# Four columns of an adaptive-norm modulation: dot products on VectorE replaced by matmuls on TensorE

## The chip, the cores and the metric

The kernel runs on one core of a Trainium2 chip. The metric is the device time of one execution in microseconds (us). A core has a matrix engine (TensorE, PE in the rows, with its weight loads shown apart as PEld), a vector engine (VectorE, DVE), a scalar engine (ScalarE, ACT), GpSimd (POOL) and a queue engine that issues most transfers (SyncE, SP).

## The reference, cut to what matters

One block of a hybrid network over 256 tokens of width 2048: a modulated norm, a large input projection, two mixers, an output projection and a feed-forward part, all in float32. What the change touches is the modulation:

```python
mod = jnp.einsum('bd,de->be', jax.nn.silu(c), w_ada[l]) + b_ada[l]      # c: [1, 2048], w_ada: [2048, 12288]
sh1, sc1, gt1, sh2, sc2, gt2 = jnp.split(mod[:, None, :], 6, axis=-1)
h = rms_norm(x, norm1_g[l]) * (1.0 + sc1) + sh1
proj = jnp.einsum('btd,dc->btc', h, w_in[l])
```

So `mod` is a vector of 12288 numbers, each a dot product of length 2048. The kernel holds it as 96 columns of 128 (`modc`, 128x96): column j (0 to 15) is `sh1` for the j-th 128 rows of the transposed activations, and column 16 + j is `sc1` for the same rows.

## The kernel before, in words

The program is written with tiles; a planner orders the instructions of each engine by a priority and by its own timeline, and each engine then runs its queue in that order. What is written under `START` comes first in priority, then the stream of weights (`STREAM`), then the rest (`MAIN`).

**Start.** `c` is loaded as one row (`crow`), spread over 128 partitions by four float32 matmuls of one row (`cps`), and turned into `sb`, a 128x2048 tile of twice silu(c), by a tanh on ScalarE and a multiply on VectorE. `x` comes transposed in four transfers (`xn`); its squares (`sqs`) are summed by float32 matmuls into `pss`, and four short VectorE steps make the reciprocal root `rs`.

**The modulation.** A column e of `modc` is one transfer of 1 MB (128 rows of the transposed `w_ada`, 8 KB each) into a slot of `ap`, and one VectorE instruction over 128x2048 elements (`ada_long`, L170 for the transfer, L158 for the dot) that multiplies by `sb` and sums. The first four columns, 0, 16, 1 and 17, have four slots of `ap` to themselves; later ones take two of these slots in turn.

**Rounds.** The input projection for 4448 of the columns of `w_in` goes in five rounds over the rows of h: rows 0 and 1 (of 16 groups of 128), then 2 and 3, then 4 to 7, and so on, so that the projection of a round needs only the columns of `modc` of its own rows. A round first makes `am` from the scale columns, then `modulate` makes each row group's `hf` on VectorE, `hhi` on ScalarE (its rounded high part) and `hlo` on VectorE (the rest), and nine groups of columns of `w_in` follow. Each step of a group loads a piece of 512 KB (`wr`, four slots), splits it into a high part on ScalarE (`whi`) and a low part on VectorE (`wlo`, three slots each), and runs three matmuls for each 128x128 tile: high by high, high by low, low by high. Between the steps the columns of `modc` for the next round are made (`next_ada`), their transfers in the same SyncE queue as the weights.

Later parts (both mixers, output projections, feed-forward) are not touched.

The lines that the change replaces, and the helper that makes a column:

```python
    rounds = [(0, 2), (2, 2), (4, 4), (8, 4), (12, 4)]
    for j in range(rounds[0][1]):
        ada_long(j)
        ada_long(16 + j)
```

Of the kernel before, what the change touches and what calls it, by code (L numbers as in the profile page):

```python
# [13 lines left out]
AF = mybir.ActivationFunctionType  # L14
OP = mybir.AluOpType
# [3 lines left out]
D = 2048  # L19
# [4 lines left out]


P_BADA, P_N1, P_N2, P_MU, P_A0, P_KK, P_KA, P_RK, P_LNW, P_LNB = 0, 96, 112, 128, 155, 163, 171, 179, 187, 195
P_QG, P_KG0, P_KG1, P_KG2, P_PEK, P_PEV, NPRM = 203, 204, 205, 206, 207, 223, 239

C_ID, C_MSK, C_HS, C_ONE, C_BLK, C_CUM, C_SEL, NCST = 0, 128, 192, 224, 225, 353, 609, 737

# [2 lines left out]
def block_kernel(ctx, tc, a):  # L33
    nc = tc.nc
# [28 lines left out]
    def B16(name, shape, dt=FT):  # L63
        return b16.tile(shape, dt, name=name, tag="b16")
# [4 lines left out]
    def RAW(name, shape):  # L69
        return rawp.tile(shape, FT, name=name, tag="raw")  # L70

    def T2(name, shape, dt=FT):
        return t2.tile(shape, dt, name=name, tag="t2")
# [4 lines left out]
    def PX(name, shape=(128, 512)):  # L78
        return px.tile(list(shape), FT, name=name, tag="px")

    def PM(name, shape=(128, 512)):
        return pmm.tile(list(shape), FT, name=name, tag="pm")
# [35 lines left out]
    xT = a["xT"].rearrange("(k p) t -> p k t", p=128)  # L118
# [4 lines left out]
    prm = cst.tile([128, NPRM], FT, name="prm")  # L123
# [8 lines left out]
    modc = cst.tile([128, 96], FT, name="modc")  # L132
# [10 lines left out]
    for i in range(4):  # L143
        ps = PM("cps")
# [11 lines left out]
    def ada_dot(r, s, start, out):  # L156
        with behind():
            V.tensor_tensor_reduce(out=r, in0=r, in1=s, scale=0.5, scalar=start,  # L158
                                    op0=OP.mult, op1=OP.add, accum_out=out)

    apb = [B16("ap0", [128, 2, D]), B16("ap1", [128, 2, D])]
    apn = [0]
    SLOTS = 2

    def ada_long(e):

        n = apn[0] if apn[0] < 4 else apn[0] % SLOTS
        r = apb[n // 2][:, n % 2]
        apn[0] += 1
        nc.sync.dma_start(r, a["w_ada_t"][e * 128:(e + 1) * 128])  # L170
        ada_dot(r, sb, prm[:, P_BADA + e:P_BADA + e + 1], modc[:, e:e + 1])
# [8 lines left out]
                    modc[:, e:e + 1] if h else part)  # L180

    rounds = [(0, 2), (2, 2), (4, 4), (8, 4), (12, 4)]
    for j in range(rounds[0][1]):
        ada_long(j)
        ada_long(16 + j)


    def split(raw, hi, lo):
# [20 lines left out]
    def parts(name, x):  # L209
        n = x.shape[0]  # L210
        r = [T2(name, [n, 512], FR) for _ in range(2)]
        split(x, r[0], r[1])
        return r
# [25 lines left out]
    def proj(segs_of, W, ms, rhi, rlo, kps, evac, banks=None, first=True, last=True):  # L239


        nb = (len(ms) + 1) // 2
        ps = banks or [PM("pp") for _ in range(nb)]
        for i, kp in enumerate(kps):
            hi, lo = weights(segs_of(kp), W)
            next_ada(ada_long if starting[0] else ada)
            todo = [[(k, m) for m in range(len(ms))] for k in range(2)]
            if 0 and i == len(kps) - 1 and nb == 2:
                todo = [[(k, m) for k in range(2) for m in range(len(ms)) if m // 2 == b] for b in range(2)]
            for part in todo:  # L250
                for k, m in part:
                    (c0, cw), kc = ms[m], 2 * kp + k
                    o = ps[m // 2][0:cw, (m % 2) * 256:(m % 2) * 256 + 256]
                    mm3(o, hi[:, k, c0:c0 + cw], lo[:, k, c0:c0 + cw], rhi[:, kc], rlo[:, kc],
                        first and i == 0 and k == 0 and m % 2 == 0, last and i == len(kps) - 1 and k == 1)
                yield
        if evac:
            with prio(STREAM):
                for b in range(nb):
                    evac(b, ps[b])  # L260
# [70 lines left out]
    w_in = a["w_in"]  # L331

    def wseg(cols):
        def of(kp):
            out, c = [], 0
            for c0, w in cols:
                out.append((w_in[kp * 256:(kp + 1) * 256, c0:c0 + w], c, w))
                c += w
            return out
        return of  # L340
# [8 lines left out]
    def acc_evac(dst, first, last):  # L349
        def f(b, ps):  # L350
            d, rows, store = dst(b)
            s = ps[0:rows, 0:d.shape[1] * 256].rearrange("p (m t) -> p m t", t=T)
            if first:
                S.copy(d, s)
            else:
                tt(d, d, s, OP.add)
            if last and store is not None:
                nc.gpsimd.dma_start(store, d)
        return f
# [4 lines left out]
    for i in (2, 3):  # L364
        groups.append(([(i * 512, 512)], 512, M4,
                       lambda b, i=i: (prk[:, i // 2, (i % 2) * 4 + 2 * b:(i % 2) * 4 + 2 * b + 2], 128, None), None))
    for i in range(2):
        groups.append(([(2048 + i * 512, 512)], 512, M4, None, pvp[2 * i:2 * i + 2]))
    for i in range(2):
        groups.append(([(i * 512, 512)], 512, M4,  # L370
                       lambda b, i=i: (prk[:, i // 2, (i % 2) * 4 + 2 * b:(i % 2) * 4 + 2 * b + 2], 128, None), None))
# [7 lines left out]
    for r, (j0, n) in enumerate(rounds):  # L379
# [9 lines left out]
        for cols, W, ms, dst, banks in groups:  # L389
            g = proj(wseg(cols), W, ms, hhi, hlo, range(j0 // 2, (j0 + n) // 2),  # L390
                     dst and acc_evac(dst, first, last), banks, first or banks is None, last or banks is None)
# [81 lines left out]
    ps = PX("gnp")  # L473
# [10 lines left out]
    for j in range(8):  # L484
        i, h = j // 4, j % 4
# [4 lines left out]
    for t in range(2):  # L490
        for h in range(2):
            ps = PX("zps")
            mm(ps, twa[:, t * 128:t * 128 + 128], w2a[:, h * 512:h * 512 + 512])
            th, cols = T2("th", [128, 512]), slice(h * 512, h * 512 + 512)
# [7 lines left out]
    for j in range(8):  # L502
        ps = PX("gps")
# [22 lines left out]
    for jp in range(4):  # L526
        ps = PX("aps")
        for i in range(2):
            j = 2 * jp + i
            mm(ps[:, i * T:i * T + T], a2[64:128, j * 128:j * 128 + 128], pl[64:128, 0], i == 0, i == 1)  # L530
        for i in range(2):
            j = 2 * jp + i
# [3 lines left out]
    ps = PX("kss")  # L536
    for jp in range(4):
        sq = T2("ksq", [128, 512])
        for i in range(2):
            j = 2 * jp + i  # L540
# [8 lines left out]
    for jp in range(4):  # L549
        ps = PX("knb")  # L550
        spread(ps, jp, nr)
        for i in range(2):
            j = 2 * jp + i
# [24 lines left out]
    for jp in range(4):  # L578
        for hh in range(2):
            ps = PX("lps")  # L580
            r0 = hh * 64
            for i in range(2):
                j = 2 * jp + i
# [19 lines left out]
    for jp in range(4):  # L603
        pb = T2("pb", [128, 2, T])
        for i in range(2):
            j = 2 * jp + i
            stt(pb[:, i], pr8[:, j], prm[:, P_RK + j:P_RK + j + 1], pk8[:, j], OP.mult, OP.mult)
        ps = PX("bps")
# [20 lines left out]
    for t in range(2):  # L629
        for jq in range(2):  # L630
            ps = PX("vps")
# [8 lines left out]
    for j in range(8):  # L640
        ps = PX("xps")
# [10 lines left out]
    for j in range(8):  # L652
        ps = PX("bkp")
# [59 lines left out]
    for c in range(8):  # L713
# [7 lines left out]
        if c:  # L721
            for hh in range(2):
                ps = PX("zps")
# [5 lines left out]
        for hh in range(2):  # L729
            ps = PX("ups")  # L730
# [5 lines left out]
        if c < 7:  # L736
            ps = PX("hps")
# [46 lines left out]
    ps = PX("fps")  # L784
# [23 lines left out]
    for jp in range(4):  # L808
        ps, pg = PX("ytp"), PX("gtp")
        ya = T2("ya", [128, 2, T])  # L810
        for i in range(2):
            j = 2 * jp + i
            for t in range(2):
                PE.transpose(ps[:, i * T + t * 128:i * T + t * 128 + 128], yn[:, t, j * 128:j * 128 + 128], ident)
        for i in range(2):
            j = 2 * jp + i
            mm(pg[:, i * T:i * T + T], g2[:, 0, j * 128:j * 128 + 128], pl[:, 1], i == 0, False)
            mm(pg[:, i * T:i * T + T], g2[64:96, 1, j * 128:j * 128 + 128], pl[64:96, 2], False, True)
        for i in range(2):
            j = 2 * jp + i  # L820
# [17 lines left out]
    ps = PX("kp")  # L838
# [4 lines left out]
    r = T2("krr", [64, 512])  # L843
    rsqrt(r, ps[0:64], 1.0 / 64, 1e-6, T2("krt", [64, 512]))
    r = parts("krp", r)
    for b in range(2):
        ps = PX("kb")
# [4 lines left out]
    for src in range(2):  # L852
        for dst in range(2):
            o = kc[dst * 64:dst * 64 + 64, src:4:2].rearrange("p g b t -> p b g t")
            i = kr[src * 64:src * 64 + 64, 4:8].rearrange("p (b g) t -> p b g t", b=2)
# [32 lines left out]
    ps = PX("c1p")  # L888
# [13 lines left out]
    ps = PX("c2p")  # L902
# [4 lines left out]
    ps, ps2 = PX("c3p"), PX("c4p")  # L907
# [12 lines left out]
    ps = PX("c5p")  # L920
# [20 lines left out]
    ps = PX("scp")  # L941
# [18 lines left out]
    ps = PX("pct")  # L960
# [132 lines left out]
    ps = PX("ss2")  # L1093
# [25 lines left out]
    for g in range(16):  # L1119
        ps = [(PM if g % 2 else PX)("pu") for _ in range(4)]  # L1120
        for kp in range(8):
# [5 lines left out]
            for k, m in order:  # L1127
                kc, c = 2 * kp + k, slice(m * 128, m * 128 + 128)
                r = h2[kc // 8][:, :, kc % 8]
                mm(ps[m].rearrange("p (x t) -> p x t", x=2), hi[:, k, c], r, kc == 0, False)  # L1130
                mm(ps[m][:, T:2 * T], lo[:, k, c], r[:, 0], False, kc == 15)
        with prio(STREAM):
            for b in range(2):
                m = 4 * g + 2 * b
                r = T2("relu", [128, 2, T])
                for i in range(2):
                    p = ps[2 * b + i]
# [5 lines left out]
    for t in range(2):  # L1143
        for q in range(4):
            ps = PX("xtp")
# [12 lines left out]
    for kp in range(32):  # L1158
# [4 lines left out]
        for k, h in ([(0, 0), (0, 1), (1, 0), (1, 1)] if kp < 31 else [(0, 0), (1, 0), (0, 1), (1, 1)]):  # L1163
                kc = 2 * kp + k
                with prio(STREAM):
                    r = RAW("wd", [128, 1024])
# [44 lines left out]
def _pack(inp):  # L1211

    g = {k: v[0] if k != "rel_bias" else v for k, v in inp.items()}
    p = np.zeros((128, NPRM), np.float32)

    def cols(at, v):
        v = v.reshape(-1, 128)
        p[:, at:at + v.shape[0]] = v.T

    cols(P_BADA, g["b_ada"])  # L1220
    cols(P_N1, g["norm1_g"])
    cols(P_N2, g["norm2_g"])
    cols(P_MU, g["rwkv_mu"][:3328])
    p[64:96, P_MU + 26] = g["rwkv_mu"][3328:]
    for at, k in ((P_A0, "rwkv_a0"), (P_KK, "rwkv_k_k"), (P_KA, "rwkv_k_a"), (P_LNW, "rwkv_ln_w"), (P_LNB, "rwkv_ln_b")):
        cols(at, g[k])
    cols(P_RK, g["rwkv_r_k"].reshape(-1))
    for at, v in ((P_QG, g["q_norm_g"]), (P_KG0, g["k_norm_g"][0]), (P_KG1, g["k_norm_g"][1]), (P_KG2, g["k_norm_g"][2])):
        p[:, at] = np.concatenate([v, v])
    for at, k in ((P_PEK, "cmp_pe_k"), (P_PEV, "cmp_pe_v")):  # L1230
        p[:, at:at + 16] = g[k].reshape(16, 2, 64).transpose(1, 2, 0).reshape(128, 16)
    c, onehot = _consts()
    out = {
        "xT": g["x"].T, "c": g["c"], "w_ada_t": g["w_ada"].T, "w_in": g["w_in"], "params": p, "consts": c,
        "onehot": onehot, "w2a": np.concatenate([g["rwkv_w2"], g["rwkv_w0"][None]]), "a2": g["rwkv_a2"],
        "g2": g["rwkv_g2"], "w1k": g["cmp_w1_k"], "w2k": g["cmp_w2_k"], "w1v": g["cmp_w1_v"], "w2v": g["cmp_w2_v"],
        "rel_bias": g["rel_bias"], "w_o_rwkv": g["w_o_rwkv"], "w_o_nsa": g["w_o_nsa"], "w_out": g["w_out"],
        "w_up": g["w_up"], "w_down": g["w_down"],
    }
    return {k: np.ascontiguousarray(v) for k, v in out.items()}  # L1240
# [17 lines left out]
```

## Time and profile before

| what | value |
|---|---|
| median of 3 runs | 1659.62 us (1655.1 to 1662.33) |
| the profiled execution | 1666.43 us, of which the span from first to last instruction is 1664.7 us |
| PE busy in the span | 1587.8 us (95%) |
| PEld busy | 1404.8 us (84%) |
| DVE busy | 1150.9 us (69%) |
| ACT busy | 757.1 us (45%) |
| mean granted TensorE clock | 0.977 of full |

Busy times are sums of the durations of an engine's instructions. Matmuls overlap in the record, so the spacing of their starts tells their rate and the duration of one does not. Only the first stretch of the span, up to some 170 us, differs from a steady flow of matmuls, and the change lies within it.

### The profile page before, as it was taken

What the parts mean: (1) busy time and instruction counts of PE and PEld (TensorE: products, weight loads), DVE (VectorE), ACT (ScalarE), POOL (GpSimd) and SP (SyncE); (2) the same over time, 40 slices, a digit from 0 to 9 for tenths busy, and PEclk for the clock granted to TensorE, in tenths of its full rate; (3) what the DMA queues carried; (4) which work ended last, traced back from release to release, by engine and by line L of the source; (5) the groups of instructions that cost most, each with busy time, mean ns of one, the idle gap of its engine ahead of it and who ended that gap; (6) DMA issues with size and microseconds to landing.
All of it is one profiled execution on the core that took longest, in us unless ns stands there. A gap on an engine that the chain in (4) does not pass through costs nothing.

```text
span 1664.7 us, 28125 instructions
## 1 busy us (share of the span) xinstructions
PE 1587.8 (95%) x11286; PEld 1404.8 (84%) x11286; DVE 1150.9 (69%) x1696; ACT 757.1 (45%) x1111; POOL 35.6 (2%) x60
## 2 busy tenths in 40 slices
PE   5969999899999989999999799999989999999998
PEld 4968998789899879877999688888878888888886
DVE  7999876977778666777876767666645555555545
ACT  4423458527323265656534444444334544444442
POOL 0000000000000000000000000000000000000001
PEclk9989999997999999999999899999999999999999
DMA  9999767674868677754787477777776556556554
GB/s 366 318 330 344 242 185 235 214 219 159 273 215 265 211 242 258 249 176 155 261 292 265 140 250 243 261 246 247 246 181 187 199 195 195 191 195 194 192 192 149
DMA packets 171190, 381.99 MB, mean 229 GB/s; under 512 B 29281, under 2 KB 43921, under 8 KB 166706
## 3 DMA queue, kind: packets, MB, share of 16 engines
q1 hardware_dynamic: 149344, 355.79, 65.4%
q0 software_dynamic: 4192, 14.17, 2.4%
q10 hardware_dynamic: 17523, 10.24, 2.1%
q8 instruction: 88, 1.44, 0.4%
q14 instruction: 43, 0.35, 0.1%
HBM read 370.13 MB, written 10.01 MB: 228 GB/s over the span
## 4 chain that ended last, share of the span: by engine, by line
PE 68%; DMA 14%; DVE 10%; ACT 3%; issue 3%; ACTq 0%; DVEq 0%; SPq 0%
PE pp L99 20%; PE pu L99 18%; PE da L99 10%; PE db L99 10%; DMA ar<-in_w_ada_t 4%; DVE wlo L90 4%; DMA wr<-in_w_in 3%; DMA wr<-in_w_out 2%; DMA wr<-in_w_up 2%; PE pvp L99 2%; ACT whi L189 1%; DVE ap L158 1%; PE y L99 1%; DVE ar L158 1%; DMA kx<-skv 1%
## 5 line engine op out<-in xcount | busy, mean ns | idle before, releaser
L189 ACT CAST whi<-wr 128x1024 fp32r<-128x1024 f32 (+1 forms) x352 | 367.1, 1044 | 522.1 <-PE pp L99 129.4
L90 DVE TENSOR_TENSOR wlo<-wr,whi 128x1024 fp32r<-128x1024 f32 (+1 forms) x352 | 426.0, 1215 | 184.8 <-ACT whi L189 181.5
L99 PE MATMUL pp<-hhi,whi 128*128 128x256 f32 (+1 forms) x1072 | 309.7, 292 | 22.1 <-ACT hhi L87 21.6
L99 PE MATMUL pp<-hhi,wlo 128*128 128x256 f32 (+1 forms) x1072 | 302.6, 290 | 6.8 <-DVE wlo L90 6.6
L99 PE MATMUL pp<-hlo,whi 128*128 128x256 f32 (+1 forms) x1072 | 307.1, 288 | 0.2 <-DVE hlo L93 0.2
L90 DVE TENSOR_TENSOR wdl<-wd,wdh 128x1024 fp32r<-128x1024 f32 x128 | 156.6, 1225 | 171.6 <-ACT wdh L189 171.6
L99 PEld LDWEIGHTS pp<-hhi,whi 128*128 128x128 f32 (+1 forms) x1072 | 209.2, 196 | 30.9 <-ACT hhi L87 22.8
L189 ACT CAST wdh<-wd 128x1024 fp32r<-128x1024 f32 x128 | 134.9, 1055 | 193.6 <-PE db L99 188.6
L99 PEld LDWEIGHTS pp<-hhi,wlo 128*128 128x128 f32 (+1 forms) x1072 | 206.0, 195 | 14.4 <-DVE wlo L90 9.7
L99 PEld LDWEIGHTS pp<-hlo,whi 128*128 128x128 f32 (+1 forms) x1072 | 209.5, 195 | 3.9 <-issue 2.7
L99 PE MATMUL pu<-h2b,whi 128*128 128x512 f32 x512 | 179.8, 399 | 4.1 <-ACT whi L189 4.1
L99 PE MATMUL pu<-h2a,whi 128*128 128x512 f32 x512 | 178.1, 399 | 4.4 <-DVE h2a L93 4.4
L99 PE MATMUL pu<-h2b,wlo 128*128 128x256 f32 x512 | 140.8, 282 | 0.5 <-DVE wlo L90 0.5
L99 PE MATMUL pu<-h2a,wlo 128*128 128x256 f32 x512 | 137.3, 282 | 0.0
L158 DVE CUSTOM_DVE_ANT_0 ar<-ar,sb,prm 128x1024 f32<-128x1024 f32 x64 | 82.0, 1282 | 67.4 <-DMA ar<-in_w_ada_t 67.4
L99 PEld LDWEIGHTS pu<-h2b,whi 128*128 128x128 f32 x512 | 96.6, 190 | 26.5 <-ACT whi L189 4.4
L99 PEld LDWEIGHTS pu<-h2a,whi 128*128 128x128 f32 x512 | 95.7, 190 | 26.1 <-DVE h2a L93 5.2
L99 PEld LDWEIGHTS pu<-h2b,wlo 128*128 128x128 f32 x512 | 96.8, 191 | 2.0 <-DVE wlo L90 1.3
L99 PEld LDWEIGHTS pu<-h2a,wlo 128*128 128x128 f32 x512 | 96.3, 191 | 2.3 <-DVE wlo L90 0.3
L158 DVE CUSTOM_DVE_ANT_0 ar<-ar,sb,adap 128x1024 f32<-128x1024 f32 x64 | 82.0, 1282 | 16.7 <-DMA ar<-in_w_ada_t 16.2
L99 PE MATMUL db<-wdl,uh 128*128 128x512 f32 x256 | 79.6, 389 | 0.0
L99 PE MATMUL db<-wdh,ul 128*128 128x512 f32 x256 | 79.6, 389 | 0.0
(336 smaller groups left out, 2747.6 us busy)
## 6 DMA issues: line engine op xcount, KB each, us to landing
wr<-in_w_in SPq DMA_DIRECT2D x136, 512.0 KB, 5.3
ar<-in_w_ada_t SPq DMA_DIRECT2D x128, 512.0 KB, 4.8
wr<-in_w_up SPq DMA_DIRECT2D x128, 512.0 KB, 4.3
wd<-in_w_down SPq DMA_DIRECT2D x128, 512.0 KB, 4.3
ap<-in_w_ada_t SPq DMA_DIRECT2D x32, 1024.0 KB, 7.0
wr<-in_w_out SPq DMA_DIRECT2D x32, 512.0 KB, 5.2
wr<-in_w_in SPq DMA_DIRECT2D x40, 256.0 KB, 3.7
wr<-in_w_o_rwkv SPq DMA_DIRECT2D x16, 512.0 KB, 4.4
```

What stands on the lines that cost most here:

```text
L90: return V.tensor_tensor(out, x, y, op=op).ins
L99: PE.matmul(out, l, r, start=start, stop=stop, skip_group_check=True)
L158: V.tensor_tensor_reduce(out=r, in0=r, in1=s, scale=0.5, scalar=start, op0=OP.mult, op1=OP.add, accum_out=out)
L189: S.copy(hi, raw)
```

## The change

The transfer of the transposed `w_ada` rows for columns 0, 16, 1 and 17 and the VectorE dots on them are replaced. The host lays the same part of `w_ada` out anew (`w_ada_p`): for each of the four columns a 128x2048 block whose 16 pieces of 128x128 have the contraction on the partitions. `c` is also put into the parameter tile as 16 columns of 128; a tanh and a multiply make `scc` (128x16), twice silu(c), with the contraction on the partitions. For each column 16 float32 matmuls follow, each with one 128x128 piece as the stationary operand and one column of `scc` as the moving one, summed in one bank of PSUM (`adp`); a VectorE instruction halves the sum and adds the bias. The transfers keep their size and their slots; `sb` is still made, as all the other columns use it.

```diff
-    for j in range(rounds[0][1]):
-        ada_long(j)
-        ada_long(16 + j)
+
+    scc = T2("scc", [128, 16])
+    act(scc, prm[:, P_C:P_C + 16], AF.Tanh, scale=0.5)
+    stt(scc, scc, 1.0, prm[:, P_C:P_C + 16], OP.add, OP.mult)
+    for i, e in enumerate((0, 16, 1, 17)):
+        r = apb[i // 2][:, i % 2]
+        apn[0] += 1
+        nc.sync.dma_start(r, a["w_ada_p"][i * 128:(i + 1) * 128])
+        ps = PX("adp")
+        for k in range(16):
+            mm(ps[:, 0:1], r[:, k * 128:k * 128 + 128], scc[:, k:k + 1], k == 0, k == 15)
+        stt(modc[:, e:e + 1], ps[:, 0:1], 0.5, prm[:, P_BADA + e:P_BADA + e + 1], OP.mult, OP.add)
...
+    cols(P_C, g["c"])
...
+        "w_ada_p": np.concatenate([g["w_ada"][:, e * 128:(e + 1) * 128].reshape(16, 128, 128).transpose(1, 0, 2).reshape(128, D)
+                                   for e in (0, 16, 1, 17)]),
```

## Rows read from the trace of the kernel before

**Rows 1.** The page, part 1: busy time, share of the span and instructions per engine.

```profile
PE 1587.8 (95%) x11286; PEld 1404.8 (84%) x11286; DVE 1150.9 (69%) x1696; ACT 757.1 (45%) x1111; POOL 35.6 (2%) x60
```

**Rows 2.** Timeline of the first 30 us: start, duration, engine, instruction, [idle before <-releaser].

```profile
2.89 7.16 PE L99 MATMUL cps<-crow,one 1*128 1x512 f32 x8 [2.89 <-DMA crow<-in_c]
...
13.66 2.34 DVE L158 CUSTOM_DVE_ANT_0 ap<-ap,sb,prm 128x2048 f32<-128x2048 f32 x1
...
16.67 2.08 PE L99 MATMUL pss<-sqs,cs 128*128 128x256 f32 x4 [6.62 <-DVE sqs L90]
...
21.88 2.34 DVE L158 CUSTOM_DVE_ANT_0 ap<-ap,sb,prm 128x2048 f32<-128x2048 f32 x1
...
25.28 0.15 DVE L93 SCALAR_TENSOR_TENSOR am<-modc,prm 128x2 f32<-128x2 f32 x1
...
27.90 1.22 PE L99 MATMUL pp<-hhi,whi 128*128 128x256 f32 x4 [9.15 <-ACT hhi L87]
...
29.28 0.58 PE L99 MATMUL pp<-hlo,whi 128*128 128x256 f32 x1 [0.16 <-DVE hlo L93]
```

**Rows 3.** DMA issues around 5.4 and 8.9 us: count, KB each, us to landing.

```profile
ap<-in_w_ada_t SPq DMA_DIRECT2D x1, 1024.0 KB, 7.5
...
ap<-in_w_ada_t SPq DMA_DIRECT2D x1, 1024.0 KB, 11.3
```

**Rows 4.** Timeline of SyncE: first issue of four, and the fourth of them alone.

```profile
5.34 3.74 SPq L170 DMA_DIRECT2D ap<-in_w_ada_t  x4
...
8.75 0.33 SPq L170 DMA_DIRECT2D ap<-in_w_ada_t  x1
```

**Rows 5.** Timeline near 653 us: 16 float32 matmuls with 32 moving columns.

```profile
653.14 3.66 PEld L99 LDWEIGHTS scp<-kcb,qn 128*128 128x128 f32 x32
```

**Rows 6.** The chain that ended last, 382 to 408 us: start, length, engine, count.

```profile
388.46 6.97 PE xps L99 x128
395.43 3.60 PE bkp L655 x16
...
405.62 1.75 PE bkp L655 x16
```

**Rows 7.** Stretches of 3.4 us: PE, PEld, DVE, ACT, POOL busy (instructions), clock, DMA share, GB/s.

```profile
382.63:386.05 3.42, 3.22 (x60) 3.21 (x61) 3.14 (x9) 3.34 (x6) 0.00 (x0) 0.50 0.02 5
...
389.46:392.87 3.41, 3.41 (x68) 3.41 (x66) 3.07 (x11) 3.30 (x7) 0.00 (x0) 0.50 0.02 5
```

**Rows 8.** Timeline of PEld: weight loads of 128x128 at 31.6 us and at 35.0 us.

```profile
31.38 0.33 PEld L99 LDWEIGHTS pp<-hhi,wlo 128*128 128x128 f32 x1
31.59 0.33 PEld L99 LDWEIGHTS pp<-hhi,whi 128*128 128x128 f32 x1
...
35.01 0.19 PEld L99 LDWEIGHTS pp<-hhi,whi 128*128 128x128 f32 x1
35.13 0.19 PEld L99 LDWEIGHTS pp<-hlo,whi 128*128 128x128 f32 x1
```

**Rows 9.** The chain that ended last around 94 us, from `am` to the first matmul.

```profile
93.98 0.17 DVE am L93
...
95.26 15.55 PE pp L99 x112
```

**Rows 10.** The chain that ended last, 29 to 92 us.

```profile
45.01 13.31 PE pp L99 x111
59.03 1.87 DVE ap L158
...
86.08 5.48 DMA ap<-in_w_ada_t
```

**Rows 11.** Longer stretches, columns as in rows 7.

```profile
20.00:28.00 8.00, 0.10 (x1) 0.10 (x1) 7.97 (x14) 3.53 (x5) 0.00 (x0) 1.00 1.07 417
...
80.00:120.00 40.00, 26.58 (x204) 26.07 (x204) 37.78 (x46) 10.88 (x13) 0.00 (x0) 0.83 0.92 327
120.00:200.00 80.00, 75.88 (x621) 74.58 (x620) 74.33 (x88) 30.48 (x35) 0.00 (x0) 1.00 0.89 307
```

More of the change, by code (lines that the diff above doesn't have):

```diff
@@ L26 @@
 P_BADA, P_N1, P_N2, P_MU, P_A0, P_KK, P_KA, P_RK, P_LNW, P_LNB = 0, 96, 112, 128, 155, 163, 171, 179, 187, 195
-P_QG, P_KG0, P_KG1, P_KG2, P_PEK, P_PEV, NPRM = 203, 204, 205, 206, 207, 223, 239
+P_QG, P_KG0, P_KG1, P_KG2, P_PEK, P_PEV, P_C, NPRM = 203, 204, 205, 206, 207, 223, 239, 255
 C_ID, C_MSK, C_HS, C_ONE, C_BLK, C_CUM, C_SEL, NCST = 0, 128, 192, 224, 225, 353, 609, 737
@@ L1233, in _pack @@
     out = {
-        "xT": g["x"].T, "c": g["c"], "w_ada_t": g["w_ada"].T, "w_in": g["w_in"], "params": p, "consts": c,
+        "xT": g["x"].T, "c": g["c"], "w_ada_t": g["w_ada"].T,
+        "w_ada_p": np.concatenate([g["w_ada"][:, e * 128:(e + 1) * 128].reshape(16, 128, 128).transpose(1, 0, 2).reshape(128, D)
+                                   for e in (0, 16, 1, 17)]),
+        "w_in": g["w_in"], "params": p, "consts": c,
         "onehot": onehot, "w2a": np.concatenate([g["rwkv_w2"], g["rwkv_w0"][None]]), "a2": g["rwkv_a2"],
```

## Prediction, made before the changed kernel was timed

> **What bounds the kernel now.** I read the page's busy shares first: PE is busy 95% of the span, VectorE 69% [rows 1]. That is an average, and the change lies wholly in the first stretch, so I went on to the timeline of the first 30 us. TensorE does its four one-row matmuls, then the four passes of `pss`, and apart from these nothing until 27.90 us, where it has waited 9.15 us for `hhi` [rows 2]. The reader is to see what stands before `hhi`: a row of VectorE dots of 2.34 us each, the first at 13.66, the fourth from 21.88 to 24.2, then `am` at 25.28, then `hf`, `hhi`, matmul [rows 2]. VectorE is busy 7.97 of the 8 us from 20 to 28 and the transfers run at 417 GB/s [rows 11].
>
> Next the landings of the four tiles of `w_ada`, which the change keeps: the first is issued at 5.34 and lands 7.5 us later, at 12.84; the fourth is issued at 8.75 and lands 11.3 us later, at 20.05 [rows 3, 4]. So the fourth dot ends some 4.1 us after its data are there: VectorE, not the transfer, sets the start of the projection, but by no more than that.
>
> Last the chain that ended last. From 29 to 58.3 us it is TensorE, then VectorE with the dots of later columns, with transfers between them (5.48 us at 86.08) until 95 us [rows 10]. From 80 to 120 us PE is busy 26.58 of 40 us while VectorE is busy 37.78 and the DMA share is 0.92 [rows 11]; from 120 to 200 PE has 4.1 us idle. A delay at the start is thus not wholly added: some of it could be taken from these gaps, if VectorE and the queue get ahead in the meantime.
>
> **Part by part: what is removed.** Four dots: 4 x 2.34 = 9.4 us of VectorE [rows 2]. None of them lies beside TensorE work; they are the path to `hhi`. The transfers stay, same size and same slots, as do `sb` and the sums for `rs`.
>
> **What is added beside other work.** `scc` needs only the parameter tile, and takes one short tanh and one short multiply of 16 columns; both can run before the first tile lands at 12.84, so I put them at nothing. If they were late, the first matmul of a column would be late by their length, under 1 us. The four sums in PSUM cost VectorE an instruction on one column each, which I price like `am`, 0.15 us [rows 2]; the first three are hidden under the next column's matmuls.
>
> **What is added on the path: 64 float32 matmuls.** Each appears as two pairs of weight load and matmul: `pss` is two matmuls in the program and x4 in the row [rows 2], `scp` 16 in the program and x32 [rows 5]. So 64 matmuls are 128 passes, each with a full 128x128 load, while only one column moves. No such matmul is in the trace. From below: `scp`, with 32 moving columns, takes 3.66 us for 32 passes, 0.114 us a pass [rows 5], at a granted clock of 1.00. From above: the transposes `bkp`, one load of 128x128 and 128 moving columns each, take 3.60 us for 16, 0.225 us, at a granted clock of 0.50, and 1.75 us, 0.109 us, in the second group, at 1.00 [rows 6, 7]. So the whole question is the clock.
>
> Low: 128 x 0.114 = 14.6 us. High: 128 x 0.225 = 28.8 us. Either way a column takes longer (3.6 or 7.2 us) than the tiles take to arrive one after the other (7.2 us for three steps, 2.4 each [rows 3, 4]), so the matmuls start at 12.84 and run on without waiting for data.
>
> I take the high end, for three rows. The projection itself starts at the low level: loads of 128x128 stand 0.21 us apart and last 0.33 us at 31.6 us, 0.12 apart and 0.19 us at 35.0 [rows 8]; the clock column prints 1.00 already for 20 to 28 us [rows 11], so there the spacing tells the level. The 7.16 us of `cps` before that, dense but with one row, had not raised it [rows 2]. And in three stretches of 3.4 us from 382.6 to 392.9 us, the first and last shown, PE is busy 3.22 and 3.41 us, PEld as well, with small matmuls, and the granted clock stays at 0.50, the 1.2 GHz level [rows 7]. A stream of loads with one moving column each looks more like these than like the dense projection that does raise it. A load that lasts 0.33 us at the low level and 0.19 us at the high one [rows 8] also says that loads follow the clock.
>
> A page speaks for the other end. The Trainium skill (TensorE: Matmul & The Clock Gate, LDWEIGHTS) gives a weight load as its columns divided by 1.2, in ns, 107 ns for 128 columns, with no clock in it. By that 128 passes would take 13.7 us, an estimate from the page, and rival "fast loads" below would hold. Rows 5 agree with it at a clock of 1.00; rows 8 speak against it at the low level.
>
> **The sum.** First landing 12.84; 128 passes at 0.225, 28.8 us: 41.6. The four passes of `pss` (2.08 us [rows 2]) share TensorE's queue; their data come after the first tile, so I count them in between: 43.7. Then the last sum's VectorE instruction, 0.15, and from `am` to the first matmul 95.26 - 93.98 = 1.28 us [rows 9]: 45.1 us. Before, this matmul stood at 27.90 [rows 2]: 17 us later; 15 if `pss` goes behind the wait of something else.
>
> What waits behind. Engines run their queues in order. The last sum's instruction stands in VectorE's queue; the `hf`, the `wlo` and the dots of columns 2 and 18 that the planner put behind it wait until 43.7 us, though their transfers have landed. ScalarE's `hhi` holds back the `whi` behind it. SyncE's next weights wait for a free slot of `wr`, the next columns for the two slots of `ap`. So most of the wait isn't used to get ahead. What is gained back: after the wait the transfers no longer run at their limit of 417 GB/s [rows 11], the next weights lie there, and the part from 58 to 95 us, where VectorE sets the chain [rows 10], starts with fewer transfers outstanding. I take 4.5 us of the 17 back, between 0 and 9 (two thirds of the 13.4 us that PE idles from 80 to 120 [rows 11], since VectorE, busy 37.78 us there, keeps the rest). Net: 17 - 4.5 = 12.5 us.
>
> The profiled execution took 1666.43 us, span 1664.7, 6.8 us above the median of 1659.62. The sum is a difference, so I put it on the median: 1659.6 + 12.5 = 1672.
>
> **Rivals.**
>
> "Slow loads" is the forecast: the low clock throughout, the queues blocked. +8 to +18 us, 1668 to 1677.
>
> "Slow loads, used wait": the same 28.8 us, but the planner has put the `wlo` and the next dots ahead of the last sum, so that VectorE and the queue are a round's work ahead when TensorE starts, and the idle 13.4 us of 80 to 120 [rows 11] is filled. For it: PE is not the bound there. Against: the slots of `wr`, `whi` and `wlo` hold only a few pieces. 17 - 12 = +5: 1665.
>
> "Fast loads": the clock rises under the narrow matmuls, or the load isn't slowed by it. 12.84 + 14.6 + 1.0 (`pss` at that rate) + 1.4 = 29.9 against 27.90, +2; if the clock is up when the projection starts, the 5 us or so that it now spends at 0.21 a matmul go at 0.12 [rows 8], -2.2. Together about 0, from -3 to +3: 1660. For it: at 1.00 the rate is on record [rows 5]. Against: rows 7. The Trainium skill (the same page, Part 1) says that the throttled state is the default and that sustained activity, not a number of matmuls, releases it; by that the clock would rise within the first column and this rival holds. Rows 7 show PE kept busy at 0.50, so here activity alone isn't enough.
>
> "VectorE relieved", the other side: faster. It needs the matmuls to keep pace with the landings, a pass under 2.4 / 32 = 0.075 us; then the last column is ready at 20.05 + 2.4, the first matmul at 24.0, 4 us earlier; the clock gives 2.2, and the VectorE time freed up to 28 us moves the splits ahead by 2 to 3. -9 us: 1651. For it: VectorE has no idle time in that stretch [rows 11] and loses 9.4 us of work. Against: the fastest full load on record is 0.109 us.
>
> **How the numbers follow.** Slow loads 0.56, slow loads with a used wait 0.14, fast loads 0.24, VectorE relieved 0.06. The likeliest gives 1672, its own range 1668 to 1677. The bound of 0.5% is 8.3 us, 1651.3 to 1667.9, about what a measurement of this kernel tells from no change. Slower: nearly all of slow loads, 0.55. Faster: 0.07. Same: 0.38. For 8 in 10 the range must reach into fast loads; I leave out its lower part, relieved VectorE, and what a changed order of the planner may add on top: 1657 to 1680.
>
> **What would show it.** In the timeline, 128 weight loads `adp`, 0.21 to 0.23 us apart, from 12.8 to about 42 us; the wait before the first `pp` at 44 to 46 us, put down to `hhi`; VectorE idle before it; in the chain, `adp` in place of the dots. The loads at 0.11 apart, or a first `pp` before 32 us, would make the forecast wrong; so would a first `pp` at 45 with PE's idle time from 60 to 170 us gone. If the span grows by far more than 17 us, the cause is elsewhere: a new order of the queues further on.

## The result and the profile after

The changed kernel takes 1680.35 us (median of 4 runs, 1677.54 to 1685.87) against 1657.44 us for the kernel before (median of 4, 1655.1 to 1662.33): a ratio of 1.0125, with a 95% interval of 1.0093 to 1.0157. It is slower by 22.9 us, or 1.25%.

The page's busy shares, for [rows 1]:

```profile
PE 1605.6 (96%) x11414; PEld 1424.2 (85%) x11414; DVE 1142.6 (68%) x1693; ACT 756.8 (45%) x1112; POOL 35.6 (2%) x60
```

PE has 128 instructions and 17.8 us more, VectorE 8.3 us less. The timeline of the first 56 us (columns as in [rows 2]) shows where they lie:

```profile
13.51 27.38 PEld L99 LDWEIGHTS adp<-scc,ap 128*128 128x128 f32 x128 [5.19 <-DVE sqs L90]
13.54 27.44 PE L99 MATMUL adp<-scc,ap 128*128 128x1 f32 x128 [3.64 <-DVE sqs L90]
...
28.74 2.35 DVE L158 CUSTOM_DVE_ANT_0 ap<-ap,sb,prm 128x2048 f32<-128x2048 f32 x1
...
34.27 2.34 DVE L158 CUSTOM_DVE_ANT_0 ap<-ap,sb,prm 128x2048 f32<-128x2048 f32 x1
...
40.84 2.05 PE L99 MATMUL pss<-sqs,cs 128*128 128x256 f32 x4
41.02 0.16 DVE L93 SCALAR_TENSOR_TENSOR modc<-adp,prm 128x1 f32<-128x1 f32 x1 [4.40 <-PE adp L99]
41.09 2.34 DVE L158 CUSTOM_DVE_ANT_0 ap<-ap,sb,prm 128x2048 f32<-128x2048 f32 x1
...
44.23 2.35 DVE L158 CUSTOM_DVE_ANT_0 ap<-ap,sb,prm 128x2048 f32<-128x2048 f32 x1
...
47.42 0.42 DVE L93 SCALAR_TENSOR_TENSOR rs<-rs,rst 128x256 f32<-128x256 f32 x1
48.26 2.35 DVE L158 CUSTOM_DVE_ANT_0 ap<-ap,sb,prm 128x2048 f32<-128x2048 f32 x1 [0.42 <-DMA ap<-in_w_ada_t]
...
50.53 1.67 DVE L93 SCALAR_TENSOR_TENSOR hf<-xn,am,rs 128x256 f32<-128x256 f32 x4
51.05 1.71 ACT L87 ACTIVATE hhi<-hf,modc 128x256 fp32r<-128x256 f32 x4 [7.19 <-DVE hf L93]
...
51.61 1.22 PE L99 MATMUL pp<-hhi,whi 128*128 128x256 f32 x4 [8.71 <-ACT hhi L87]
...
54.93 0.58 PE L99 MATMUL pp<-hlo,whi 128*128 128x256 f32 x1 [2.10 <-DVE hlo L93]
```

The reader is to see three things. The 128 passes take 27.38 / 128 = 0.214 us each and run without a gap, though the tiles have long landed. `pss`, which the norm needs, stands behind all of them (40.84, before 16.67 [rows 2]), so `rs` is ready only at 47.8. And VectorE, free again at 41.2, first does three dots of later columns, which stand ahead of `hf` in its queue; two more were done beside the passes, from 28.7 and 34.3 us, so that five dots of later columns are behind it when the projection starts, where the kernel before has done none. The first matmul of the projection comes at 51.61 instead of 27.90 [rows 2]: 23.7 us later.

How much of that is left later? I read both kernels at three marks: the first `pp`, the last `aps` (a small matmul just behind the projection's rounds), and the first `ss` (the second norm, behind both mixers and the output projections). Each kernel has two profiled executions here, the second from the experiments below.

| kernel | first `pp` | last `aps` | first `ss` | `aps` to `ss` | span |
|---|---|---|---|---|---|
| before | 27.90 | 277.5 | 930.4 | 652.9 | 1664.7 |
| before, second | 28.19 | 280.7 | 926.8 | 646.1 | 1658.1 |
| changed | 51.61 | 289.8 | 946.3 | 656.5 | 1675.8 |
| changed, second | 51.85 | 291.6 | 948.8 | 657.2 | 1683.3 |

In the means of the pairs the changed kernel is 23.7 us late at the first `pp`, 11.6 at the last `aps`, 19.0 at `ss` and 18.2 at the end. So half of the delay is made up within the projection, and 7.3 us come on top in the mixers, a stretch that differs by 6.8 us between the two executions of the kernel before. That the medians lie 23 us apart and these spans 18 is the spread of the executions: the first profile of before took 1666.43 us, 9 above its median.

How the half is made up shows in the stretch from the first `pp` to 170 us (columns as in [rows 7]), here of the kernel before:

```profile
27.90:170.00 142.10, 123.65 (x968) 121.22 (x969) 131.39 (x150) 52.77 (x66) 0.00 (x0) 0.95 0.94 335
```

and of the changed one:

```profile
51.61:170.00 118.39, 110.51 (x873) 108.64 (x873) 115.30 (x133) 48.46 (x62) 0.00 (x0) 0.99 0.96 342
```

PE idles 142.10 - 123.65 = 18.5 us before and 7.9 us after. The granted clock is 0.95 and 0.99 there; both figures leave out the low level at the start of the projection, which the column prints as 1.00. The projection starts later but has fewer holes, and above all it lacks one: the wait for `hhi` at the start of the third round, which in the kernel before is (PE's waits from 52 to 170 us: total us, times, longest)

```profile
PE pp L99 <- ACT hhi L87: 12.4, 1, 12.4
```

and 14.6 us in its second execution. In the changed kernel no wait of PE from 60 to 170 us is longer than 3.5 us in either execution.

The mixers' stretch has the same matmuls in both, but more PE idle time. Of the second execution of before:

```profile
280.70:926.80 646.10, 625.79 (x5830) 561.88 (x5828) 484.95 (x906) 311.81 (x531) 26.20 (x46) 0.98 0.72 231
```

and of the changed kernel:

```profile
291.60:948.80 657.20, 626.85 (x5831) 563.82 (x5830) 483.87 (x906) 310.99 (x530) 26.21 (x46) 0.97 0.71 227
```

20.3 us idle against 30.4, with the busy times of PE and of VectorE equal within 1.1 us. The amount of work is the same; what differs is waiting.

### The profile page after: what moved, and what is told of

It reads as the page before. It is cut to its first block, busy times and chain, and to the rows that moved or that the text cites. A ratio compares the mean times of both kernels' runs of the same rounds, so it can differ in the third digit from the quotient of the medians.

```text
span 1675.8 us, 28381 instructions
## 1 busy us (share of the span) xinstructions
PE 1605.6 (96%) x11414; PEld 1424.2 (85%) x11414; DVE 1142.6 (68%) x1693; ACT 756.8 (45%) x1112; POOL 35.6 (2%) x60
## 4 chain that ended last, share of the span: by engine, by line
PE 62%; issue 22%; DMA 8%; DVE 6%; ACT 2%; POOL 1%; SPq 0%; DVEq 0%; ACTq 0%; POOLq 0%
PE pu L99 19%; PE pp L99 14%; PE da L99 10%; PE db L99 10%; DMA ar<-in_w_ada_t 2%; PE pvp L99 2%; DVE wlo L90 2%; DMA wr<-in_w_out 2%; PE adp L99 2%; DVE ap L158 1%; PE po L99 1%; ACT whi L198 1%; DMA wr<-in_w_up 1%; PE sps L99 1%; DMA gate<-sma 1%
## 5 line engine op out<-in xcount | busy, mean ns | idle before, releaser
L158 DVE CUSTOM_DVE_ANT_0 ar<-ar,sb,adap 128x1024 f32<-128x1024 f32 x64 | 81.8, 1278 | 17.8 <-DMA ar<-in_w_ada_t 17.5
```

## Experiments

All ratios are against the kernel before on the same chips, whose median was 1656.5 to 1658.7 us there. Each kernel was timed beside its own runs of the kernel before, so two of them are best compared by their ratios.

**Half of the pieces.** The sum over 8 of the 16 pieces, so half of it is left out.

```diff
-        for k in range(16):
-            mm(ps[:, 0:1], r[:, k * 128:k * 128 + 128], scc[:, k:k + 1], k == 0, k == 15)
+        for k in range(8):
+            mm(ps[:, 0:1], r[:, k * 128:k * 128 + 128], scc[:, k:k + 1], k == 0, k == 7)
```

> Each of the four columns is summed from 8 of its 16 pieces, so half of the sum is left out; transfers, slots and all other instructions stay. Theory A (the matmuls lie on the path to the projection, 0.214 us for each of 128 passes): 64 passes fewer, adp ends near 27 us instead of 41, the first pp at 37 to 40 us instead of 51.6, and the time falls by 10 to 14 us from 1680, to about 1667 to 1670. Theory B (the loss comes from the new order of the instructions behind the start, as the planner makes another one for any change): the time stays near 1680 or moves by an amount that has nothing to do with the 13.7 us.

1674.68 us, 1.0098 (1.0069 to 1.0126): 5.7 us less than the changed kernel by the medians and 4.5 by the ratios, with intervals that overlap; not 10 to 14. The first `pp` came at 37.96, 13.7 us earlier, as theory A has it; the last `aps` at 285.4, only some 5 us earlier. So a microsecond at the start is worth less than half of one at the end of the projection. Theory A holds for the start and falls for the size at the end; theory B alone can't explain an `aps` that moves with the start.

**`pss` ahead.** The loop of matmuls and its four VectorE instructions are moved, in the program, behind the matmuls of `pss`; the transfers stay.

```diff
     for k in range(2):
         mm(pss, ones, sqs[:, k], k == 0, k == 1)
+    for i, e in enumerate((0, 16, 1, 17)):
+        r = apb[i // 2][:, i % 2]
+        ps = PX("adp")
...
```

> The matmuls of the four columns are written behind pss, so that pss goes ahead of them in TensorE's queue; nothing is left out. Theory A1 (the order around the matmuls costs beside the matmuls: pss behind all 128 passes and three dots of later columns ahead of hf): rs is ready near 20 us, the first pp at 43.5 to 45.5 us instead of 51.6, the time falls by 4 to 7 us, to about 1675. Theory A0 (only the 27.4 us of passes count, what stands around them is made up later): the first pp is earlier, the time stays within 2 us of 1680.

1674.47 us, 1.0099 (1.0074 to 1.0123). First `pp` at 45.76, last `aps` at 284.8. The order around the matmuls cost 6 us at the first `pp` and 5 to 7 at the last `aps`, theory A1; of the whole time 4 us by the ratios, with intervals that overlap. Three dots of later columns were done before the first `pp`, and the wait of the third round is gone, as in the changed kernel. The mixers' stretch is 660.8 us.

**Dots behind, too.** As above, and every later dot is issued behind the `hlo` of the first round.

```diff
-        with behind():
+        with (tc.issue_after(first_h[0]) if first_h else behind()):
             V.tensor_tensor_reduce(out=r, in0=r, in1=s, scale=0.5, scalar=start,
...
             lasth = modulate(j0, n, xn)
             if first:
+                first_h.append(lasth)
```

> As the one with pss ahead, and the VectorE dots of all later columns are also issued behind hlo of the first round; nothing is left out. Theory A1: first pp near 44 us and the dense projection near 45.5, time 1672 to 1675, as the sum of the prediction has it. Theory C (the dots done during the wait are what the kernel lives from later, the used wait): with them moved behind, the first matmul is as early but the time is no better than with pss ahead alone, 1675 or more.

1670.07 us, 1.0081 (1.0055 to 1.0108). Its timeline is the sum of the prediction nearly row for row:

```profile
43.36 0.16 DVE L93 SCALAR_TENSOR_TENSOR modc<-adp,prm 128x1 f32<-128x1 f32 x1 [6.67 <-PE adp L99]
43.55 0.16 DVE L93 SCALAR_TENSOR_TENSOR am<-modc,prm 128x2 f32<-128x2 f32 x1
...
44.83 1.22 PE L99 MATMUL pp<-hhi,whi 128*128 128x256 f32 x4 [1.51 <-ACT hhi L87]
```

But the wait is now unused. From 30 to 60 us (columns as in [rows 7]; the clock column prints 1.00 although the passes in this stretch have the price of the low level):

```profile
30.00:60.00 30.00, 28.49 (x176) 28.41 (x177) 15.14 (x19) 7.70 (x12) 0.00 (x0) 1.00 0.51 185
```

VectorE is busy 15.14 us and the transfers run at 185 GB/s; with `pss` ahead alone the same stretch has

```profile
30.00:60.00 30.00, 26.91 (x142) 26.39 (x143) 21.64 (x29) 6.61 (x12) 0.00 (x0) 1.00 0.80 284
```

What wasn't done then is missing later: the wait for `hhi` of the third round is back,

```profile
PE pp L99 <- ACT hhi L87: 11.8, 1, 11.8
```

and the last `aps` comes at 293.1 instead of 284.8. That is theory C, as far as the projection goes. The time is no worse all the same (1.0081 against 1.0099, with intervals that overlap), because the mixers' stretch is 649.4 us here and 660.8 there. Theory A1 came out for the first matmul, theory C for the projection, and neither for the time: 1672 to 1675 and 1675 or more were expected.

**Only `scc`.** The parameter columns and `scc` stay, the dots come back.

```diff
-    for i, e in enumerate((0, 16, 1, 17)):
...
+    for j in range(rounds[0][1]):
+        ada_long(j)
+        ada_long(16 + j)
```

> scc, the 16 extra parameter columns and their two instructions are there, but the four columns are made by VectorE dots as before; nothing is left out. Theory A: within 3 us of the kernel before, 1655 to 1662, first pp near 28 us. Theory B (any change of the start re-plans the rest and that alone costs): 1665 or more although the first pp is as early as before.

1660.81 us, 1.0023 (1.0003 to 1.0044), first `pp` at 26.70, `aps` to `ss` 649.6. A new plan that begins alike costs some 4 us here, by the interval 0.5 to 7; that is a little more than theory A's 3 us, and theory B by itself isn't the 23.

**Dense matmuls ahead, to raise the clock.**

```diff
+    wj = PM("wj")
+    for i in range(8):
+        mm(wj, ident, xn[:, 0:2], True, True)
     for i, e in enumerate((0, 16, 1, 17)):
```

> Eight dense float32 matmuls of 128x128 by 512 columns, whose result nobody reads, stand between cps and the first matmul of the four columns; all else stays. They take TensorE from about 10 to about 20 us and so start the four columns some 6 us later. Theory L (the pass takes 0.214 us because the clock is low; a load follows the clock): the clock rises in the dense matmuls, the passes then take 0.11 us as long as it stays up, adp ends at 34 to 36 us instead of 41, and the time falls by 2 to 4 us from 1680. Theory N (0.214 us is the price of a load with one moving column at any clock): adp ends near 47, time 1683 to 1687. In between, if one moving column can't hold the clock up: the first passes at 0.11, the later ones at 0.214.

1677.33 us, 1.0107 (1.0070 to 1.0145). Weight loads of `adp` in two windows, 19 to 24.5 and 25.5 to 41 us (min/median/max ns, first and last start):

```profile
L99 PEld LDWEIGHTS adp<-scc,ap x49: 190/192/192, 19.1 to 24.5; 128*128 128x128 f32 x49
...
L99 PEld LDWEIGHTS adp<-scc,ap x74: 333/333/333, 25.4 to 40.9; 128*128 128x128 f32 x74
```

and the stretches, with the granted clock as third number from the end:

```profile
22.00:24.00 2.00, 2.00 (x20) 2.00 (x19) 0.92 (x2) 1.09 (x2) 0.00 (x0) 1.00 1.04 386
24.00:25.00 1.00, 1.00 (x9) 1.00 (x10) 0.36 (x2) 0.73 (x1) 0.00 (x0) 0.83 1.05 387
25.00:26.00 1.00, 1.00 (x6) 1.00 (x6) 0.99 (x1) 0.96 (x1) 0.00 (x0) 0.50 1.12 430
...
30.00:40.00 10.00, 10.00 (x49) 10.00 (x48) 5.88 (x6) 0.00 (x0) 0.00 (x0) 0.50 0.80 299
```

Until 24.5 us a pass takes (24.5 - 19.1) / 48 = 0.113 us at a clock of 1.00; then the clock falls to 0.50, the 1.2 GHz level, in the midst of passes that leave PE and PEld no idle time, and a pass takes (40.9 - 25.4) / 73 = 0.212 us. The expectation's third case came: the price is that of the clock, and this stream of loads with one moving column didn't hold the clock up. Theory N falls. `adp` ended at 41, no later than without the dense matmuls, although it began 5 us later. The first `pp` came at 54.24, as three dots of later columns stand ahead of `hf` here too, and the last `aps` at 295.2; the time differs from that of the changed kernel by less than the intervals.

**One column by matmul.** Column 0 only, the other three by dots, `pss` ahead.

```diff
-    for i, e in enumerate((0, 16, 1, 17)):
-        r = apb[i // 2][:, i % 2]
-        apn[0] += 1
-        nc.sync.dma_start(r, a["w_ada_p"][i * 128:(i + 1) * 128])
...
+    r0 = apb[0][:, 0]
+    apn[0] += 1
+    nc.sync.dma_start(r0, a["w_ada_p"][0:128])
+    for e in (16, 1, 17):
+        ada_long(e)
...
```

> Only column 0 is made by matmuls (32 passes), columns 16, 1 and 17 by VectorE dots as before; pss is ahead of the matmuls; nothing is left out. Theory A (what counts is how late the first pp is): 32 passes end near 24 us, beside the dots, so the first pp stands at 26 to 28.5 us as before and the time is within 3 us of the kernel before, 1655 to 1661. Theory B (a new order of the rest costs by itself): 1665 or more with the first pp as early as before.

1653.63 us, 0.9973 (0.9953 to 0.9993): faster than the kernel before, and below both theories. So I timed it again:

> The one-column kernel unchanged, timed again against the kernel before. Theory G (its lead of 0.3% is real): 1650 to 1656, ratio under 1 with its interval again. Theory Z (it was chance): 1655 to 1660, interval around 1.

1654.30 us in 12 runs, 0.9971 (0.9951 to 0.9990). Theory G: the lead of 0.3% is real. The timeline of the second:

```profile
16.78 7.16 PEld L99 LDWEIGHTS adp<-scc,ap 128*128 128x128 f32 x32
...
21.99 2.34 DVE L158 CUSTOM_DVE_ANT_0 ap<-ap,sb,prm 128x2048 f32<-128x2048 f32 x1
...
25.46 0.15 DVE L93 SCALAR_TENSOR_TENSOR am<-modc,prm 128x2 f32<-128x2 f32 x1
```

The 32 passes end at 23.9 us, beside the third dot, and cost nothing; VectorE has a dot fewer. The first `pp` comes at 26.82, and from there to 170 us PE idles 15.4 us instead of 18.5; the wait for `hhi` of the third round is 9.5 us (9.3 in the first run), where the kernel before has 12.4 and 14.6 and the one with only `scc` 14.2. The last `aps` is at 273.9 us (273.8), 3.6 to 6.9 earlier than before.

**Two columns.** Columns 0 and 16, with the same edit.

> Columns 0 and 16 are made by matmuls (64 passes, whole sums), columns 1 and 17 by VectorE dots; pss is ahead; nothing is left out. Theory A (what counts is how far the matmuls outlast the dots): 64 passes of 0.214 us from 17 to 31 us, first pp at 32 to 34, some 5 us later than before; about half of that is closed later by PE's idle gaps, so the projection ends 2 to 4 us later than in the kernel before and the time is 1657 to 1664 if the order of the mixers is one of the good ones, 7 more if not. Theory G (what the one-column kernel gained is VectorE time, and more columns gain more): 1648 to 1653.

1656.36 us, 0.9987 (0.9966 to 1.0007): no difference that can be measured. First `pp` at 32.19, last `aps` at 281.1, about as before. Theory A for the start and, within a microsecond, for the time; G's "more columns gain more" falls: the second column's passes already outlast the dots.

**Both kernels again, for a second profile each.**

> The kernel before, unchanged, for a second profiled execution. Theory: what stands out in the first one, a single transfer of 15.3 us at 1207 us in the feed-forward part, is an accident of that execution and is not here; up to the end of the projection the two agree within 2 us; time 1653 to 1662.

1659.87 us. The expectation falls: the slow transfer is there again, 13.71 us long at 1201.78, and one of 13.53 us stands in the changed kernel as well, so it belongs to the program and is no accident. The projection ended at 280.7 instead of 277.5, 3.2 us apart and not the 2 that I expected; that is the spread against which the table is to be read.

> The changed kernel, unchanged, for a second profiled execution. Theory: adp again at 0.214 us a pass and the first pp near 51.6 us, as they hang on nothing that varies; time 1677 to 1686; what differs from the first execution lies behind the projection.

1685.11 us, first `pp` at 51.85. The table above has the rest.

**Four slots for later columns.** One line in each kernel:

```diff
-    SLOTS = 2
+    SLOTS = 4
```

> The changed kernel, with four slots instead of two for the tiles of all later columns; nothing is left out. Theory U (during the wait for the matmuls the transfers stand still because the two slots are taken, and a used wait is given back later): more dots done before the first pp, DMA above the 274 GB/s of the changed kernel from 30 to 60 us, the projection ends 2 to 6 us earlier than at 290, time 1672 to 1678. Theory O (slots don't hold it): end of the projection within 2 us of the changed kernel.

> The kernel before, with four slots instead of two for the later columns; nothing is left out. Theory U: there is no long wait to use, so the projection ends within 3 us of 277 to 281 and the time within 4 us of 1657. Rival: the two slots hold the stream in the kernel before as well, and the time falls to 1650 or less.

1696.15 us, 1.0226 (1.0194 to 1.0258), for the changed kernel, and 1675.87 us, 1.0104 (1.0071 to 1.0137), for the one before: both 16 to 17 us slower than with two slots. Theory U falls, and so do the other two. In the changed kernel with four slots more dots are done before the first `pp` (seven instead of five, the last of them just begun) and the transfers from 30 to 60 us do run faster,

```profile
30.00:60.00 30.00, 17.48 (x75) 16.28 (x76) 21.97 (x31) 2.71 (x6) 0.00 (x0) 1.00 0.99 375
```

375 GB/s against 274, but the last `aps` comes at 304.7 instead of 289.8. What PE waits for from 52 to 170 us (total us, times, longest) in the kernel before with four slots shows a part of the reason:

```profile
PE pp L99 <- DVE wlo L90: 12.9, 8, 2.6
PE pvp L99 <- DVE wlo L90: 4.6, 2, 3.3
```

With two slots they are shorter:

```profile
PE pp L99 <- DVE wlo L90: 4.5, 4, 2.2
```

By 100 us VectorE has begun 21 dots and 19 `wlo` with four slots, and 17 and 21 with two: it does dots of columns that are needed late ahead of the `wlo` that is needed now. So the two slots ration the dots. The wait of the third round is gone with four slots, but all waits together are 23.6 us in this stretch against 18.1 with two.

## Why the prediction was right, and where its sum was off

The direction, the price of a pass and its reason came out. The size came out short: 12.5 us and 1672 were forecast and 22.9 us and 1680.35 measured. That is beyond the 1668 to 1677 given for the likeliest case (whose +18 us make 1678) and at the very end of the whole range, in the part left open for what a changed order of the planner may add. Of the signs named, the 128 loads came as described, from 13.5 to 40.9 us; a first `pp` at 44 to 46 us and an idle VectorE before it did not.

**The price of a pass.** 0.225 us was taken, 0.214 came. That it is the low clock's price was argued from [rows 7, 8] and is now shown by the dense matmuls ahead: same matmuls, 0.113 us at 1.00 and 0.212 at 0.50. (The clocks given for `scp` and `bkp` are not in the rows beside them, but the trace has them: 1.00 from 653.14 us, 0.50 from 395.43, 1.00 from 405.62.) The formula for a load without a clock in it (the Trainium skill, TensorE: Matmul & The Clock Gate, LDWEIGHTS), which gives 107 ns for 128 columns, fits the first and not the second; the measurement decides. The dense matmuls ahead had the clock at 1.00 when the passes began; the passes kept PE and PEld busy without a gap, and under them it fell to 0.50, and without the dense matmuls it stayed at the low level for all 27 us. The Trainium skill (TensorE: Matmul & The Clock Gate, Part 1) says that activity releases the throttle; these passes, with PE and PEld busy all the time, didn't release it, so the measurement decides here too.

**The first matmul.** The sum said 45.1 us, the changed kernel has 51.61. The step that failed is "what waits behind": I listed the dots behind the last sum, and the planner had put three of them, and the four steps of `rs`, between the last sum and `hf`. With `pss` ahead and the dots behind, the sum's own order, it is 44.83. (The prediction also says that none of the four removed dots lies beside TensorE work; `pss` lies beside the second one, for 2.08 us [rows 2].)

**What is gained back.** 4.5 of 17 us was taken, 9 at most. Measured at the end of the projection: 12.1 of 23.7. The dots done before the first matmul are the reason: they are the used wait of the second rival, whose 12 us this is. They take away the third round's wait of 12.4 to 14.6 us, part of the idle time that the prediction had counted [rows 11]; without them (dots behind) the wait is 11.8 us and only little comes back, 45 - 28 = 17 late at the start and 14 at the last `aps`. The statement that most of the wait isn't used to get ahead failed with that. The net there, 11.6, is near the predicted 12.5 by luck, from two terms that were each off by about the same.

**What lay outside the sum.** It ended with the projection. The mixers add 7.3 us, a term I had put at nothing and left to the range. The stretch from `aps` to `ss` took 644.7 to 652.9 us in eight executions (the kernel before twice, only `scc`, dots behind, dense matmuls ahead, one column twice, two columns) and 649.6 with four slots in the kernel before, but 656.5 to 661.1 in the changed kernel twice, with half of the pieces, with `pss` ahead and with four slots in the changed kernel. It isn't lateness: with the dense matmuls ahead the last `aps` is later (295.2) than in the changed kernel and the stretch takes 649.5 us. Busy times are equal, so the planner's order is the likely reason, but that isn't shown: no run held the order fixed, and the long ones don't lose their time at one place. The first `po`, a matmul further on in the mixers, comes 418 us behind the last `aps` in both executions of the changed kernel, but 400 us with half of the pieces and with `pss` ahead, and 396 to 411 in the nine executions with a short stretch. What was said ahead of the prediction, that only the first 170 us differ from a steady flow of matmuls, was too strong: PE idles 20 us in this stretch of the kernel before.

**The rivals.** "Fast loads" fell with the pass. "VectorE relieved" named an effect that can come under another condition: not a pass under 0.075 us, but passes that end before the dots beside them. At one column of four that holds, and the kernel gains 0.3%. That the gain is VectorE's time is likely from the shorter wait of the third round; as a new plan alone moved the time by some 4 us (only `scc`), it isn't proved.

| columns by matmul | passes | first `pp` | wait of the third round | last `aps` | median us | ratio |
|---|---|---|---|---|---|---|
| 0 (only `scc`) | 0 | 26.70 | 14.2 | 279.5 | 1660.81 | 1.0023 |
| 1, second timing | 32 | 26.82 | 9.5 | 273.9 | 1654.30 | 0.9971 |
| 2 | 64 | 32.19 | 8.3 | 281.1 | 1656.36 | 0.9987 |
| 4, `pss` ahead | 128 | 45.76 | none | 284.8 | 1674.47 | 1.0099 |
| 4, the change | 128 | 51.61 | none | 289.8 | 1680.35 | 1.0125 |

The rows with one and two columns have `pss` ahead, so the fourth row is the one to compare them with.

## What to carry to other kernels

A matrix times a vector puts the matrix through the weight loads, and at the start of this kernel these ran at the low clock: price it by the load (0.21 us for 128x128 of a float32 pass, two passes a matmul), not by its one column. Work moved from a full engine to an idle one gained here as long as it ended beside what remained: one column of four, and not all four. When a long job enters an engine's queue, look at what the planner puts behind it and ahead of the next needed step, there and on the engines that wait: here that cost 6 us at the first matmul. And ask what the waiting engines do in the meantime: the dots done during the wait gave back half of the delay.

## What the hardware showed that I had not expected

That the granted clock fell while PE and PEld showed no idle time at all: 1.00 until about 24.5 us, 0.50 from 25 us on, in one unbroken stream of 128x128 loads with one moving column, begun at 19.1 us behind dense matmuls. A busy share of 100% did not keep TensorE at 2.4 GHz here.
